# Turning exponentials by a product with diag(1/sum), and the norms' factors moved from x into the weights, in a ten-stage fp32 transformer program

## The chip, the core and the metric

The program runs on one core of one Trainium2 chip. The metric is device time in microseconds of a whole execution. The kernel before takes 2619.73 us, the median of three runs (2615.45 to 2620.55 us). The execution that the profiler recorded took 2619.76 us; its span, from the first instruction to the last, is 2617.6 us. The mean granted clock of TensorE over that span is 0.982 of full speed.

## The reference

Two blocks of two transformer layers run one after the other over 256 tokens of 1024 features, all in fp32. In the first block a context of 256 tokens is carried along with the latent ones through the first layer. What matters here are the attentions, since in each of them a matrix of exponentials is normalised by its row sums and multiplied by values. Cut to that:

```python
# first block, layer 0 (mixer_ab): two attentions over 256 tokens and 256 context tokens
y_x = concat([attention(qa, [ka, ka_c], [va, va_c], 64 ** -0.5),      # 8 heads, 2 K/V heads, 64 wide
              attention(qb, [kb, kb_c], [vb, vb_c], 96 ** -0.5)])     # 8 heads, 96 wide, latent K/V
y_c = the same for the context's queries over the context's keys
# layer 1 (mixer_cd): a gated recurrence, and attention over an 8x16 window of the grid plus the context
p   = softmax(concat([q @ k_win * scale + bias, q @ k_ctx * scale]))
# second block, layer 0: three branches of sparse attention, 12 heads in 3 groups, and 4 memory heads
out = g[0] * softmax(q @ k_cmp) @ v_cmp + g[1] * softmax(q @ k_sel) @ v_sel + g[2] * softmax(q @ k_win) @ v_win
mem = softmax(q_mem @ k_mem * scale) @ v_mem                          # 256 memory tokens
# layer 1: K and V from one norm of x, the queries from another
k_s, v_s = split(rmsnorm(x, kv_norm) @ w_kv_shared)
q, q_mem = split(rmsnorm(x, attn_norm[1]) @ b_w_in)                   # three dilation patterns, 8 heads
out = sum over the patterns of (softmax(q_i @ k_i) @ v_i) weighted by softmax(logsumexp_i)
mem = as above
```

Here `rmsnorm(x, g) = x * rsqrt(mean(x^2) + eps) * g`. Between the mixers stand feed-forward blocks (SwiGLU 2816 wide in the first block, squared ReLU 4096 wide in the second).

## The kernel before

**Stages.** The program is ten stages in a row: modulation with the first feed-forward, `mixer_ab`, a feed-forward, another, `mixer_cd`, the opening of the memory, a feed-forward, the sparse mixer with its memory attention, an MLP, the dilated mixer with its memory attention, an MLP. The residual `xr` stays transposed in SBUF, with the features on the partitions, in eight chunks of 128.

**Products.** A large product is done in three products of rounded parts (`mm3`, lines 328 to 330): high by high, high by low, low by high. `split` makes the two halves, a cast on ScalarE (L300) and a subtraction on VectorE (L301). Weights come by DMA into `raw` (three buffers, issued on SP's queue) and are split into tiles `wh` and `wl` of up to 512 columns, nine of each. `proj_steps` (L719) runs a projection: for each tile of 128 tokens it collects eight chunks of 1024 features in a PSUM bank and then calls `evict`.

**Exponentials.** `softmax` (L836) takes scores of 128 queries from a PSUM bank `at`: the row maxima on VectorE (L841), the exponentials with their row sums on ScalarE (L848), the reciprocal of the sums and then the scaling of each row block by it on VectorE (L859). The scaled block `P` lies with queries on the partitions. `attend_steps` turns it by TensorE transposes of 128x128 against the identity `ident` (L888) into the bank where the scores stood; the result is copied to `PT` by ScalarE or VectorE in turn (L896, L898) and multiplied by the values (`po`, L904). The score product of a head pair is L880, and L810 is the helper `transposes` (its transpose is L814), which turns any list of blocks. The window attention does the same with four blocks of 128 per head (L934, values at L945). In the sparse mixer two maps per head are scaled, `np` (the window's branch on the earlier keys) on POOL and `P` on VectorE (L2030), by gate over sum, and are then turned (L2040 to L2044). In the dilated mixer POOL adds the three patterns' exponentials (L2251, L2252), VectorE scales the sum (L2255), and `transposes` turns it.

**The dilated mixer's input.** Before its projections `gain_split` (L1605) runs 16 times, one ScalarE copy with a factor (L1608) and one VectorE operation (L1609) of 256 columns each: eight chunks times two norms' gains. The tokens multiplied by the gain of the keys' norm lie in columns 256 to 511 of `xh` and `xl`, those of the queries' norm in columns 0 to 255. The root-mean-square factor is applied when a projection is evicted. The projections come in the order `d_k`, `d_q0`, `d_q1`, `d_q2`, `d_qm` (memory queries, 256 columns), `d_v`.

**Order.** The mixers' code is written as generators; a main stream of projections or output products calls `step`, which runs the other stream (a pair of heads, say) up to its next `yield`. This sets the order in which instructions are recorded. The framework then places them on the engines' queues, in which each engine runs in order. Tiles come from pools of rings: a tile name with n buffers makes the instruction that fills buffer n+1 wait for the last reader of buffer 1.

## Time and profile before

| | us |
|---|---|
| median of three runs | 2619.73 (2615.45 to 2620.55) |
| the profiled execution, whole | 2619.76 |
| its span, first to last instruction | 2617.6 |
| TensorE busy in it | 2504.4 (96%) |
| VectorE busy | 1794.8 (69%) |
| ScalarE busy | 1255.3 (48%) |
| POOL busy | 408.5 (16%) |

The engines run beside one another, so these do not add up to the span. A busy engine is not one that sets the end: that is read from the chain of waits, which goes back from the last instruction to what released it, and so on. Both are averages over ten stages with different limits, so the views used below are cut to stretches: the first mixer's pairs run at 450 to 650 us, the window attention at 1550 to 1690, the memory attention of the sparse mixer within 1900 to 1950, the sparse attention at 1980 to 2110, the dilated mixer's projections at 2320 to 2360 and its pairs with the second memory attention at 2360 to 2430. An F32 product of two plain tiles can leave more records in the trace than instructions in the code, so both are counted below.

### The profile page before, as it was taken

The numbers are of one execution on the slowest core, as the hardware profiler recorded it, in microseconds if no ns is written. First come the engines' busy times: TensorE is split into PE (matmuls) and PEld (weight loads), VectorE is DVE, ScalarE is ACT, GpSimd is POOL, SyncE is SP. The second block draws the span as 40 slices with busy tenths as digits, with TensorE's granted clock in tenths as the row PEclk, the third lists the DMA queues.
The fourth block names the chain that finished last, engine by engine and source line by source line (L and its number), as shares of the span: only waits on it lengthen the run. The fifth ranks groups of instructions, "written<-read, shape, count | busy, mean of one in ns | idle before, by whom it ended". The sixth has DMA issues, their size and how long they took to land.

```text
span 2617.6 us, 40598 instructions
## 1 busy us (share of the span) xinstructions
PE 2504.4 (96%) x14835; PEld 2158.1 (82%) x14835; DVE 1794.8 (69%) x3656; ACT 1255.3 (48%) x2641; POOL 408.5 (16%) x457
## 2 busy tenths in 40 slices
PE   6999999999999999999999999889998899988999
PEld 3888888877888888788888887789986789977999
DVE  4999536786998335843336578866677776788764
ACT  3332235665423234233235668555555655665653
POOL 3000004201200003000003234220022211232111
PEclk8999999999999999999999999989998999999999
DMA  7777332110675333843333221346662255542554
GB/s 268 232 234 234 122 96 67 55 60 30 210 237 180 97 97 125 290 131 97 97 97 105 89 81 45 98 136 197 185 189 74 85 181 182 185 142 69 182 184 143
DMA packets 114472, 367.21 MB, mean 140 GB/s; under 512 B 13600, under 2 KB 23776, under 8 KB 112864
## 3 DMA queue, kind: packets, MB, share of 16 engines
q1 hardware_dynamic: 114272, 364.61, 43.4%
q8 instruction: 117, 1.92, 0.3%
q14 instruction: 83, 0.68, 0.1%
HBM read 363.51 MB, written 1.05 MB: 139 GB/s over the span
## 4 chain that ended last, share of the span: by engine, by line
PE 72%; DVE 12%; issue 5%; ACT 5%; DMA 4%; POOL 3%; SPq 0%; POOLq 0%; DVEq 0%; ACTq 0%
PE ps L329 21%; PE ps L330 21%; PE ps L328 21%; DVE wl L301 2%; DVE prod L446 2%; DMA raw<-w 1%; PE po L904 1%; PE at L880 1%; POOL acc L520 1%; PE at L888 1%; ACT wh L300 1%; PE at L814 1%; DMA ident<-c_ident 1%; DVE xl L569 1%; DVE nu L562 1%
## 5 line engine op out<-in xcount | busy, mean ns | idle before, releaser
L300 ACT CAST wh<-raw 128x512 fp32r<-128x512 f32 (+3 forms) x1064 | 637.3, 608 | 914.8 <-PE ps L329 750.6
L301 DVE TENSOR_TENSOR wl<-raw,wh 128x512 fp32r<-128x512 f32 (+3 forms) x1064 | 740.4, 704 | 426.8 <-ACT wh L300 411.7
L328 PE MATMUL ps<-xh,wh 128*128 128x256 f32 (+1 forms) x2384 | 793.8, 336 | 16.9 <-ACT xh L300 5.0
L329 PE MATMUL ps<-xl,wh 128*128 128x256 f32 (+1 forms) x2384 | 796.5, 335 | 10.4 <-POOL xl L573 3.8
L330 PE MATMUL ps<-xh,wl 128*128 128x256 f32 (+1 forms) x2384 | 792.6, 333 | 0.9 <-DVE wl L301 0.9
L328 PEld LDWEIGHTS ps<-xh,wh 128*128 128x128 f32 x2384 | 456.2, 193 | 64.0 <-ACT xh L300 7.1
L329 PEld LDWEIGHTS ps<-xl,wh 128*128 128x128 f32 x2384 | 458.4, 192 | 59.1 <-DVE xl L569 7.2
L330 PEld LDWEIGHTS ps<-xh,wl 128*128 128x128 f32 x2384 | 458.3, 192 | 44.1 <-DVE wl L301 2.1
L328 PE MATMUL ps<-hh,wh 128*128 128x256 f32 (+1 forms) x1312 | 416.5, 318 | 3.7 <-ACT hh L300 3.7
L329 PE MATMUL ps<-hl,wh 128*128 128x256 f32 (+1 forms) x1312 | 416.6, 318 | 0.7 <-DVE hl L301 0.6
L330 PE MATMUL ps<-hh,wl 128*128 128x256 f32 (+1 forms) x1312 | 416.0, 317 | 0.0
L520 POOL TENSOR_TENSOR acc<-acc,sq 128x256 f32<-128x256 f32 x119 | 100.4, 846 | 1375.7 <-ACT sq L519 1371.2
L446 DVE CUSTOM_DVE_ANT_0 prod<-aw,crow,adab 128x1024 f32<-128x1024 f32 x224 | 286.8, 1280 | 7.8 <-DMA aw<-ada_t 5.6
L328 PEld LDWEIGHTS ps<-hh,wh 128*128 128x128 f32 x1312 | 248.0, 189 | 21.7 <-ACT hh L300 4.6
L329 PEld LDWEIGHTS ps<-hl,wh 128*128 128x128 f32 x1312 | 247.9, 189 | 18.7 <-DVE hl L301 1.7
L330 PEld LDWEIGHTS ps<-hh,wl 128*128 128x128 f32 x1312 | 247.9, 189 | 16.8
L328 PE MATMUL ps<-wh,xh 128*128 128x512 f32 (+4 forms) x464 | 180.4, 389 | 1.5 <-ACT xh L1608 1.5
L329 PE MATMUL ps<-wl,xh 128*128 128x512 f32 (+4 forms) x464 | 177.9, 384 | 3.5 <-DVE wl L301 3.5
L330 PE MATMUL ps<-wh,xl 128*128 128x512 f32 (+4 forms) x464 | 176.9, 382 | 0.3 <-DVE xl L1609 0.3
L592 DVE SCALAR_TENSOR_TENSOR xr<-ps,hgate,xr 128x256 f32<-128x256 f32 x168 | 75.5, 479 | 74.4 <-PE ps L330 73.8
L329 PEld LDWEIGHTS ps<-wl,xh 128*128 128x128 f32 x464 | 88.7, 191 | 20.2 <-DVE wl L301 6.5
L300 ACT CAST hh<-s 128x256 fp32r<-128x256 f32 (+1 forms) x158 | 76.9, 487 | 57.5 <-DVE s L642 49.0
(496 smaller groups left out, 2702.8 us busy)
## 6 DMA issues: line engine op xcount, KB each, us to landing
raw<-w SPq DMA_DIRECT2D x240, 512.0 KB, 3.7
aw<-ada_t SPq DMA_DIRECT2D x128, 512.0 KB, 4.1
raw<-m_up SPq DMA_DIRECT2D x64, 512.0 KB, 3.6
raw<-m_down SPq DMA_DIRECT2D x64, 512.0 KB, 3.5
raw<-w SPq DMA_DIRECT2D x32, 384.0 KB, 4.0
row<-ada_w SPq DMA_DIRECT2D x8, 1024.0 KB, 12.9
raw<-d_q SPq DMA_DIRECT2D x12, 512.0 KB, 4.0
raw<-ab_g SPq DMA_DIRECT2D x8, 512.0 KB, 3.6
```

The lines of the kernel that those rows point to most:

```text
L300: self.nc.scalar.copy(h, src)
L301: self.nc.vector.tensor_tensor(l, src, h.bitcast(F32), op=ALU.subtract)
L328: mm(out, lh, rh, start=start, stop=False)
L329: mm(out, lh, rl, start=False, stop=False)
L330: mm(out, ll, rh, start=False, stop=stop)
L446: v.tensor_tensor_reduce(prod, w, self.crow[:, s], 1.0, self.adab[:, l, j : j + 1], op0=ALU.mult, op1=ALU.add, accum_out=self.mods[l][:, m ...
L520: self.nc.gpsimd.tensor_tensor(acc, acc, t, op=ALU.add)
L562: nc.vector.scalar_tensor_tensor(u, self.xr[half][:, k], a[:, k : k + 1], rb, op0=ALU.mult, op1=ALU.mult)
L569: nc.vector.scalar_tensor_tensor(l, u, b[:, k : k + 1], h.bitcast(F32), op0=ALU.add, op1=ALU.subtract)
L592: self.nc.vector.scalar_tensor_tensor(x, pt, gate[:, d : d + 1], x, op0=ALU.mult, op1=ALU.add)
L814: self.nc.tensor.transpose(pt[:rows, n * P : (n + 1) * P], x, self.ident)
L880: nc.tensor.matmul(o, s, kp, start=n == 0, stop=n == len(passes) - 1)
```

## The change

`softmax` no longer scales the exponentials. It calls `diagonals`, which makes for each row block a 128x128 tile `dg`, the identity with 1/sum in its diagonal, as a copy on ScalarE with a scale per partition. `turn` is a plain F32 product of the block (stationary) with that diagonal (moving); the result is the block turned and scaled at once. All transposes of exponentials in the four mixers and both memory attentions become such products, and the scalings on VectorE, and POOL's in the sparse mixer, go. In the sparse mixer a diagonal holds gate over sum. There are 160 diagonals and 384 turns: 192 turns in the first mixer, 64 in the window attention, 16 in each memory attention, 72 in the sparse and 24 in the dilated one.

The `dg` tiles are a new ring: 5 buffers of 128 columns in the first mixer, 3 of 128 in the second, 4 of 256 in the sparse and in the dilated one. Tables of the rotary embedding (`tq`, `tk`), and in the sparse mixer four small tiles of the compression, now lie in that ring too.

In the dilated mixer x is split once, without a gain, into columns 0 to 255: eight casts and eight subtractions in place of 16 and 16. The two norms' gains go into the weights: `weight(gain=...)` makes the high part as a ScalarE copy with the gain as factor and the low part by one VectorE operation, weight times gain minus high part. The features of a weight chunk lie on the partitions, so the factor is one number per partition. That holds for all the mixer's projections, 40 splits of 512 columns and 8 of 256. The weights of `d_qm` are now cut in tiles of 256 columns and not of 512, so that each tile has one gain.

```diff
+    def weight(self, ap, cut=512, gain=None):
...
-            self.split(h, l, r[:, c0 : c0 + m])
+            if gain is None:
+                self.split(h, l, r[:, c0 : c0 + m])
+            else:
+                g = gain[:, c0 // cut : c0 // cut + 1]
+                self.nc.scalar.activation(h, r[:, c0 : c0 + m], AF.Copy, scale=g)
+                self.nc.vector.scalar_tensor_tensor(
+                    l, r[:, c0 : c0 + m], g, h.bitcast(F32), op0=ALU.mult, op1=ALU.subtract
+                )
...
-        ws = [self.weight(u, 512 // ncols * ncols) for u in units]
         kp = kc // len(units)
+        if gain is None:
+            ws = [self.weight(u, 512 // ncols * ncols) for u in units]
+        else:
+            ws = [self.weight(u, ncols, gain[:, kp * n : kp * n + kp]) for n, u in enumerate(units)]
...
         nc.vector.reciprocal(z[:, 2 : 2 + nq], z[:, :nq])
-        for j in range(nq):
-            c = slice(j * nk, (j + 1) * nk)
-            nc.vector.tensor_scalar(pt[:, c], pt[:, c], z[:, 2 + j : 3 + j], None, op0=ALU.mult)
+        return self.diagonals(z[:, 2 : 2 + nq])
+
+    def diagonals(self, z):
+        n, per = z.shape[-1], self.DG_COLS // P
+        ds = []
+        for j in range(n):
+            if j % per == 0:
+                t = self.mw.tile([P, self.DG_COLS], F32, name="dg", tag="dg", bufs=self.DG_BUFS)
+            ds.append(t[:, j % per * P : (j % per + 1) * P])
+            self.nc.scalar.activation(ds[-1], self.ident, AF.Copy, scale=z[:, j : j + 1])
+        return ds
+
+    def turn(self, out, x, d):
+        self.nc.tensor.matmul(out, x, d, start=True, stop=True)
...
-                            nc.tensor.transpose(
-                                tp[:, c : c + P], p[:, j * nk + kk * P : j * nk + (kk + 1) * P], self.ident
-                            )
+                            self.turn(tp[:, c : c + P], p[:, j * nk + kk * P : j * nk + (kk + 1) * P], ds[j])
...
-                        self.bmul(p0, p0, z[:, 8:10])
-                        for b in range(2):
-                            nc.vector.tensor_scalar(p1[:, b], p1[:, b], z[:, 10 + b : 11 + b], None, op0=ALU.mult)
+                        ps.append((p0, p1, self.diagonals(z[:, 8:12])))
...
         for k in range(KC):
-            for g, c0 in ((12, 256), (7, 0)):
-                self.gain_split(self.xr[0][:, k], k, self.gv[:, g], c0)
+            self.split(self.xh[:, k, :256], self.xl[:, k, :256], self.xr[0][:, k])
+        gkv, gq = self.gv[:, 12], self.gv[:, 7]
...
                     nc.vector.reciprocal(z[:, 2:4], z[:, 0:2])
-                    for t, x in enumerate(pp):
-                        nc.vector.tensor_scalar(x[:, 0], x[:, 0], z[:, 2 + t : 3 + t], None, op0=ALU.mult)
+                    ds.append(self.diagonals(z[:, 2:4]))
...
-                    ta = self.transposes([pp[0][:, 0], pp[1][:, 0, :P], pp[1][:, 0, P:]])
+                    ta = self.psum(tag="at")[:, : 3 * P]
+                    for n, (x, d) in enumerate(((pp[0][:, 0], d0), (pp[1][:, 0, :P], d1), (pp[1][:, 0, P:], d1))):
+                        self.turn(ta[:, n * P : (n + 1) * P], x, d)
...
-            self.proj(self.units("d_k"), 512, (2, 3), heads(kx, "k", tk, kd))
+            self.proj(self.units("d_k"), 512, T2, heads(kx, "k", tk, kd), gain=gkv)
...
-                self.proj_steps(self.units("d_qm"), 256, T2, ev_m),
-                self.proj_steps(self.units("d_v"), 512, (2, 3), ev_v),
+                self.proj_steps(self.units("d_qm"), 256, T2, ev_m, gain=gq),
+                self.proj_steps(self.units("d_v"), 512, T2, ev_v, gain=gkv),
```

How instructions stand on the engines is shown at three places. First TensorE in the first mixer, where a projection (`ps`, from split weights `wh`, `wl` and tokens `xh`, `xl`) runs between the steps of the first head pair; `at` is the bank of scores and turned blocks. Before:

```order
L328 MATMUL ps<-wh,xh 128x416
L329 MATMUL ps<-wl,xh 128x416
L330 MATMUL ps<-wh,xl 128x416
L888 MATMUL at<-ident,P 128x128 x4
L880 MATMUL at<-q_3903,q_4029 128x512 x2
L328 MATMUL ps<-wh,xh 128x416
L888 MATMUL at<-ident,P 128x128 x4
L329 MATMUL ps<-wl,xh 128x416
```

And of the change:

```order
L336 MATMUL ps<-wh,xh 128x416
L337 MATMUL ps<-wl,xh 128x416
L338 MATMUL ps<-wh,xl 128x416
L888 MATMUL at<-dg,P 128x128 x4
L909 MATMUL at<-q_3905,q_4031 128x512 x2
L888 MATMUL at<-dg,P 128x128 x4
L336 MATMUL ps<-wh,xh 128x416
```

The turned blocks stand where the transposes stood; the second group of four moved one projection product ahead, and nothing else did. One row is one instruction of the code.

Second ScalarE in the sparse mixer, at the first pair of heads of a group. `np` and `P` are the exponentials of the two maps, `pcT` and `PT` the copies of turned blocks out of PSUM. Before:

```order
L1977 ACTIVATE pc<-pc 128x8x16
L2021 ACTIVATE np_19209,ssum<-np_19209,smax,rq_18309 128x128
L2021 ACTIVATE P,ssum<-P,smax,rq_18309 128x256
L2021 ACTIVATE np_19209,ssum<-np_19209,smax,rq_18309 128x128
L2021 ACTIVATE P,ssum<-P,smax,rq_18309 128x256
L2034 COPY pcT<-at 128x256
L2021 ACTIVATE np_19231,ssum<-np_19231,smax,rq_18309 128x128
L2021 ACTIVATE P,ssum<-P,smax,rq_18309 128x256
L2021 ACTIVATE np_19231,ssum<-np_19231,smax,rq_18309 128x128
L2021 ACTIVATE P,ssum<-P,smax,rq_18309 128x256
L2045 COPY PT<-at 128x512
```

And of the change, the same pair:

```order
L2004 ACTIVATE pc<-pc 128x8x16
L2047 ACTIVATE np_19295,ssum<-np_19295,smax,rq_18391 128x128
L2047 ACTIVATE P,ssum<-P,smax,rq_18391 128x256
L2047 ACTIVATE np_19295,ssum<-np_19295,smax,rq_18391 128x128
L2047 ACTIVATE P,ssum<-P,smax,rq_18391 128x256
L2047 ACTIVATE np_19320,ssum<-np_19320,smax,rq_18391 128x128
L883 ACTIVATE dg<-ident,ssum 128x128 x4
L2047 ACTIVATE P,ssum<-P,smax,rq_18391 128x256
L2047 ACTIVATE np_19320,ssum<-np_19320,smax,rq_18391 128x128
L2047 ACTIVATE P,ssum<-P,smax,rq_18391 128x256
L2058 COPY pcT<-at 128x256
L2067 COPY PT<-at 128x512
```

The four diagonals of the first head now stand behind the first exponential of the second head, so three exponentials and the two copies come after them; four more diagonals, of the second head, follow the last row shown.

Third ScalarE in the dilated mixer, where the memory queries (`qm`) are evicted and the weights of the values (`wh`, the 512-wide casts) are split. Before:

```order
L300 CAST wh<-raw 128x512
L833 CAST qT_22948<-at 64x512
L300 CAST wh<-raw 128x512
L755 ACTIVATE rsy<-ss_23384,cols 128x8
L2170 ACTIVATE qm<-ps,rms 128x256
L756 ACTIVATE rsy<-rsy 128x8
L744 ACTIVATE ps<-ps,rms 128x256
L300 CAST wh<-raw 128x512 x4
L2170 ACTIVATE qm<-ps,rms 128x256
L744 ACTIVATE ps<-ps,rms 128x256
L300 CAST wh<-raw 128x512
```

And of the change:

```order
L848 CAST qT_23053<-at 64x512
L756 ACTIVATE ps<-ps,rms 128x512
L322 ACTIVATE wh<-raw,gv 128x512
L848 CAST qT_23054<-at 64x512
L767 ACTIVATE rsy<-ss_23490,cols 128x8
L768 ACTIVATE rsy<-rsy 128x8
L2192 ACTIVATE qm<-ps,rms 128x256
L756 ACTIVATE ps<-ps,rms 128x256
L322 ACTIVATE wh<-raw,gv 128x512 x4
L2192 ACTIVATE qm<-ps,rms 128x256
L756 ACTIVATE ps<-ps,rms 128x256
L322 ACTIVATE wh<-raw,gv 128x512 x3
```

One more cast of the value weights stands six rows above the first piece, so three of the eight stood ahead of the first eviction of `qm`, four between the two, and one behind. Of the change one stands ahead, four between and three behind. The rows of 512 columns with the factor `gv` are those same splits.

## Rows read from the trace of the kernel before

**Rows 1.** The page: busy time by engine, and the chain that ended last by engine.
```profile
PE 2504.4 (96%) x14835; PEld 2158.1 (82%) x14835; DVE 1794.8 (69%) x3656; ACT 1255.3 (48%) x2641; POOL 408.5 (16%) x457
...
PE 72%; DVE 12%; issue 5%; ACT 5%; DMA 4%; POOL 3%; SPq 0%; POOLq 0%; DVEq 0%; ACTq 0%
```

**Rows 2.** Seven stretches: length, busy us per engine (instructions), TensorE clock, DMA.
```profile
450.00:650.00 200.00, 193.33 (x1135) 152.03 (x1134) 151.07 (x379) 123.73 (x295) 30.61 (x46) 1.00 0.14 45
1550.00:1690.00 140.00, 127.19 (x858) 104.30 (x857) 117.48 (x238) 102.14 (x243) 43.43 (x40) 0.98 0.19 59
1900.00:1950.00 50.00, 49.51 (x308) 42.20 (x306) 36.13 (x100) 25.17 (x53) 13.36 (x18) 1.00 0.59 188
1980.00:2110.00 130.00, 109.20 (x673) 86.33 (x673) 100.60 (x318) 79.76 (x219) 31.23 (x34) 0.89 0.26 82
2260.00:2300.00 40.00, 40.00 (x296) 37.95 (x295) 28.58 (x57) 24.05 (x47) 12.13 (x13) 1.00 0.57 182
2320.00:2360.00 40.00, 36.14 (x192) 29.77 (x191) 38.83 (x76) 27.99 (x61) 13.75 (x10) 1.00 0.40 129
2360.00:2430.00 70.00, 61.69 (x409) 50.29 (x408) 57.47 (x179) 44.48 (x112) 24.98 (x39) 0.99 0.22 69
```

**Rows 3.** Chain of waits by line: 450:650, 1550:1690, 1980:2110, 2320:2360, 2360:2430.
```profile
by line: PE po L904 16.0%; PE ps L328 14.3%; PE ps L329 13.7%; PE ps L330 13.5%; PE at L880 13.0%; PE at L888 10.0%; PE at L814 4.7%; DVE smax L841 2.3%; ACT P L848 1.4%; DVE P L859 1.1%; issue 0.8%; DVE wl L301 0.7%; DVE q L834 0.7%; DVE P
...
by line: issue 5.7%; DVE AT L1472 5.6%; DVE f L1447 4.9%; DVE smax L841 4.4%; PE at L1458 3.9%; PE ps L330 3.8%; PE ps L328 3.7%; PE ps L329 3.5%; PE po L945 3.5%; ACT t L1256 3.1%; ACT t L1258 2.9%; ACT t L1257 2.8%; ACT P L848 2.5%; PE at
...
by line: PE ps L328 6.6%; PE ps L329 6.5%; PE ps L330 5.9%; PE at L1958 5.5%; PE po L2056 5.0%; ACT P L2021 4.3%; issue 4.1%; ACT np L2021 4.0%; PE po L2053 3.9%; PE at L1999 3.9%; ACT xh L1608 3.1%; ACT wh L300 3.0%; DVE wl L301 3.0%; PE a
...
by line: DVE wl L301 34.0%; DVE qT L834 15.6%; issue 10.8%; DVE ss L745 8.4%; DVE x L778 5.2%; DVE P L797 5.0%; DVE x L773 4.8%; DVE kT L301 4.7%; DVE x L805 4.3%; DVE ss L757 3.0%; DVE rsy L345 1.8%; DVE rsa L344 1.4%; DVE rsa L343 1.3%; A
...
by line: issue 13.7%; POOL acc L520 7.9%; DMA raw<-m_up 7.7%; POOL dp L2252 7.4%; PE at L2233 7.2%; POOL dp L2251 6.8%; DVE dp L2239 6.2%; DVE wl L301 5.7%; DMA raw<-d_wout 3.7%; ACT wh L300 3.4%; PE po L904 3.2%; ACT xh L1608 2.9%; PE po L
```

**Rows 4.** TensorE by form: shapes, xcount | busy us, mean ns | idle before.
```profile
L888 PE MATMUL at<-ident,P 128*128 128x128 f32 x224 | 35.0, 277 | 4.4 <-DVE P L859 3.6 <-ACT P L848 0.2
...
L1458 PE MATMUL at<-f,kk 128*128 128x128 f32 x256 | 34.4, 277 | 0.8 <-DVE AT L1472 0.8
```

**Rows 5.** Timeline of TensorE: start us, us from first start to last end, xcount.
```profile
1477.66 0.61 PE L1458 MATMUL at<-f,kk 128*128 128x128 f32 x4
...
1568.14 0.60 PE L934 MATMUL at<-ident,P 128*128 128x128 f32 x4
```

**Rows 6.** Waits of TensorE, 450:650: us in total, times, longest.
```profile
PE at L888 <- DVE P L859: 2.1, 3, 1.2
```

**Rows 7.** VectorE by form, the scalings by 1/sum.
```profile
L859 DVE TENSOR_SCALAR P<-P,ssum 128x512 f32<-128x512 f32 x48 | 24.9, 518 | 1.0
...
L859 DVE TENSOR_SCALAR P<-P,ssum 128x256 f32<-128x256 f32 x48 | 16.0, 376 | 0.4
...
L2030 DVE TENSOR_SCALAR P<-P,ssum 128x256 f32<-128x256 f32 x24 | 11.6, 526 | 0.3
...
L2255 DVE TENSOR_SCALAR dp<-dp,ssum 128x128 f32<-128x128 f32 x8 | 4.0, 498 | 0.5 <-POOL dp L2252 0.3
...
L2255 DVE TENSOR_SCALAR dp<-dp,ssum 128x256 f32<-128x256 f32 x8 | 3.5, 432 | 2.3 <-POOL dp L2252 2.3
```

**Rows 8.** ScalarE by form, the nearest to a diagonal.
```profile
L2021 ACT ACTIVATE np<-np,smax,rq 128x128 f32<-128x128 f32 x24 | 11.7, 486 | 6.4 <-DVE smax L2015 5.0 <-DVE ssum L2025 1.4
...
L1448 ACT ACTIVATE kk<-f,sides 128x256 f32<-128x256 f32 x32 | 16.2, 513 | 2.8 <-PE at L1458 1.3 <-DVE f L1447 1.2
...
L519 ACT ACTIVATE sq<-xr 128x256 f32<-128x256 f32 x105 | 42.8, 413 | 55.5 <-DVE xr L592 40.6 <-POOL acc L520 7.9 <-DVE ssv L531 2.3
...
L1423 ACT COPY state<-at 128x64 f32<-128x64 f32 x8 | 1.7, 213 | 4.0 <-PE at L1416 4.0
```

**Rows 9.** VectorE by form: a weight's low part, and a low part with a factor.
```profile
L301 DVE TENSOR_TENSOR wl<-raw,wh 128x512 fp32r<-128x512 f32 x984 | 701.0, 719 | 418.9 <-ACT wh L300 404.1 <-PE ps L330 7.2
...
L1552 DVE SCALAR_TENSOR_TENSOR q<-at,gqk,q 128x512 fp32r<-128x512 f32 x4 | 3.0, 746 | 0.4 <-ACT q L1551 0.4
```

More of the change, by code (lines that the diff above doesn't have):

```diff
@@ L758, in rstd_heads, with rope_tabs @@
         return self.newton(y, a, ss)
-    def rope_tabs(self, pool, name, tab, g, gs, scale):
+    def rope_tabs(self, pool, name, tab, g, gs, scale, bufs=None, whole=False):
         hd = tab.shape[-1]
-        o = pool.tile([P, 2, 2, hd], F32, name=name)
+        if whole or bufs is None:
+            o = pool.tile([P, 2, 2, hd], F32, name=name, tag=name, bufs=bufs or 1)
+        else:
+            o = [pool.tile([P, 2, hd], F32, name=name, tag=name, bufs=bufs) for _ in range(2)]
         for j, gg in enumerate((g, gs)):
             self.nc.vector.scalar_tensor_tensor(
-                o[:, j], tab[:, j], scale, gg.unsqueeze(1).to_broadcast([P, 2, hd]), op0=ALU.mult, op1=ALU.mult
+                o[:, j] if whole or bufs is None else o[j], tab[:, j], scale, gg.unsqueeze(1).to_broadcast([P, 2, hd]), op0=ALU.mult, op1=ALU.mult
             )
@@ L1914, in compress @@
                 nc.vector.tensor_tensor(kc, kc, tcmp[:, 0], op=ALU.mult)
-                kc2 = mw.tile([64, 2, 64], F32, name="kc2")
+                kc2 = tile("dg", [256], 4)[:64, :P].rearrange("p (b c) -> p b c", b=2)
                 for b in range(2):
```

58 lines of the change are left out of this document (27 added, 31 removed).

## The prediction

> **What bounds the kernel now.** I read the page first: TensorE is busy 96% of the span and makes up 72% of the chain that ended last, VectorE 12% of it [rows 1]. That is an average over stages, so the next view was busy time by stretch [rows 2], for the places where exponentials are turned: the first mixer's pairs (450 to 650 us), the window attention (1550 to 1690), the two memory attentions (in 1900 to 1950, and in 2360 to 2430), the sparse attention (1980 to 2110) and the dilated one (2360 to 2430). Last I read the chain of waits of those stretches alone [rows 3]. The reader is to see that they have different limits:
>
> - First mixer: seven TensorE rows hold 16.0 + 14.3 + 13.7 + 13.5 + 13.0 + 10.0 + 4.7 = 85.2% of the chain. The turning itself (L888) is 10.0% of 200 us. TensorE idles 6.7 us of 200. Paced by TensorE.
> - Window attention: VectorE and ScalarE rows of the recurrence stand between TensorE rows of under 4% each. Paced by hops between engines.
> - Sparse attention: the listed TensorE rows make up 37% of the chain, the exponentials on ScalarE 8.3%, and the rest is spread. The granted clock is 0.89 [rows 2].
> - Projections of the dilated mixer (2320 to 2360): VectorE is busy 38.83 of 40 and holds nearly the whole chain, 34.0% of it in splitting weights.
> - Dilated pairs: POOL's sums of exponentials (L2251, L2252) are 14.2%, and the scaling waits for them [rows 3, 7].
>
> **What an edit costs.** *A turn.* The transposes of lines 888, 934 and 2040 to 2044, and those of the dilated pairs (by the helper of line 814), become 384 products of F32 with a diagonal: 192 in the first mixer, 64 in the window attention, 32 in the memory attentions (16 and 16), 72 in the sparse and 24 in the dilated one. A transpose leaves one record: L888 stands 224 times in the trace, as often as the code issues it. A product of two F32 tiles leaves two: L1458 issues 4 pairs x 8 levels x 4 = 128 products of this form, and the trace has 256 records of the same shape and the same 277 ns [rows 4]. Four records in a row take 0.60 us as transposes and 0.61 us as product halves, so each further one costs (0.61 - 0.28) / 3 = 0.11 us either way [rows 5]. A turn as a product is thus one record longer, and all of them together are 384 x 0.11 = 42 us of TensorE work, an upper end if nothing hides it. The chain gives the same price from the other side: 20.0 us for 192 transposes is 0.104 us each [rows 3].
>
> The Trainium skill, page "TensorE: Matmul & The Clock Gate", section Terms, says that the transpose mode is 4 times as fast for FP32. By that a turn would gain three records and not one. The two records of L1458 say two times; the rule has its own rival below.
>
> *A scaling that goes.* VectorE loses 48 x 518 + 48 x 376 + 24 x 526 + 8 x 498 + 8 x 432 ns = 63 us as means, of which the rows count 24.9 + 16.0 + 11.6 + 4.0 + 3.5 = 60 us as busy [rows 7]; by stage 28.6 us in the first mixer, 8.3 in the window attention, 12.6 in the sparse one, 7.4 in the dilated one, 6.0 in the memory attentions. But TensorE waited for it little: 2.1 us in the whole first mixer [rows 6].
>
> *A diagonal that comes.* The trace has none. ScalarE's nearest rows are a 128x64 copy without a scale pointer at 213 ns (below) and a 128x128 exponential with its sum at 486 ns (above). A scale pointer costs 513 - 413 = 100 ns at 256 columns [rows 8]; the copy plus 64 columns at (413 - 213) / 192 ns plus the pointer gives 0.38. I take 0.4 us, 160 times: 64 us of ScalarE, 26 of them in the first mixer, 19 in the sparse attention, 6.4 each in the window attention, the dilated pairs and the memory attentions. It starts after the same reciprocal that the scaling followed. For a 512-wide row 0.4 takes the place of 0.518. For a sparse head four diagonals (1.6 us, one after the other) take the place of two VectorE scalings (1.05 us) beside POOL's. What is queued behind a waiting diagonal is the next exponential and the PSUM copies that turned tiles wait for.
>
> **The sum, stage by stage.**
>
> - First mixer: 20.0 us of transposes double, and 85.2% of the chain is TensorE, so 0.852 x 20.0 = 17.0; the rest fits into waits that exist. The scaling's 1.1% of the chain goes: -2.2. Place by place the turns stand in the queue where the transposes stood, so nothing moves to a better place. **+15** (between -2 and +21).
> - Window attention: 64 x 0.11 = 7.0 on TensorE, 6.4 on ScalarE, which is already busy 102 of 140, and 8.3 off VectorE, busy 117 of 140. Each is on the chain part of the time. **+2** (-8 to +13).
> - Memory attention before the sparse one: 16 turns in a stretch where TensorE is busy 49.51 of 50: **+1.8**; the second one goes with the dilated pairs.
> - Sparse attention: 72 x 0.11 = 7.9 at 37% of the chain is +2.9; 19 us of ScalarE at 14% (L2021, L1608, L300) is +2.7; 12.6 us of VectorE at about a quarter is -3.1. **+2.5** (-13 to +27).
> - The eight saved splits of x: 8 of the 16 pairs of one ScalarE and one VectorE operation. They fall in 2260 to 2300, where TensorE is busy 40.00 of 40 [rows 2]. **0**; the cover is the tail of the MLP and the products of the first key columns. Without it they would be worth one 256-wide operation each, 8 x 0.5 = -4.
> - The weights' factors: 40 splits 512 wide and 8 of 256 in place of 4 of 512. A low part with a factor takes 746 ns against 719 [rows 9], though the first reads PSUM; I take +50 ns, 40 x 0.05 = 2 us on the engine that paces 2320 to 2360, and 1 us for four operations more. Then there is a wait: the memory queries now fill 8 of the 9 weight buffers and not 4, so the value columns' splits move back. ScalarE's order shows one of eight ahead of the first query eviction where three stood, and three behind the second where one stood. Two splits of 0.72 us late is about 1. **+4** (0 to +8).
> - Dilated pairs with the second memory attention: the scaling no longer stands between POOL's sum and the turn, 0.43 to 0.5 us for each of 16 tiles in four overlapping pairs, against 40 x 0.11 = 4.4 of TensorE. **-2** (-10 to +5).
>
> That is 15 + 2 + 1.8 + 2.5 + 0 + 4 - 2 = +23.3. The profiled execution took 2619.76 us around a span of 2617.6, and the median of the runs is 2619.73, so the sum needs no correction: **2643 us**.
>
> **The rivals.**
>
> - *VectorE is the bound of the attentions (faster).* For it: 117 of 140 and 100.6 of 130 us busy in the window and the sparse attention [rows 2]. If the 8.3, 12.6 and 7.4 us all come off the path, the time is 2620 - 28.3 + 15 + 1.8 + 4 = 2612. It decides from the point where the freed time of VectorE on the chain exceeds TensorE's 17 us in the first mixer. Against it: TensorE's waits name the scaling for 2.1 us there [rows 6]. 0.14.
> - *TensorE's extra records fit into its waits (no change).* The first mixer has 14.8% of 200 = 29.6 us of chain off TensorE, more than 20. For that the waits would have to come when turns are ready; they come in front of them. Then +0 to +4: 2620 to 2624. 0.13.
> - *ScalarE's queue ends last (slower still).* Its diagonals wait in order for VectorE's reciprocal and hold back exponentials. All 42 us of TensorE show and 6 to 7 more from the sparse and window attentions: 2619.8 + 42 + 7 = 2669. 0.17.
> - *A transpose is four times as fast as a product:* 384 x 3 x 0.11 = 127 us more TensorE, 85% of it seen: about 2728. The 256 records of L1458 speak against it. 0.01. The page named above has the rule.
> - *The change does not do what it says:* products with a diagonal run as one record. Then only the VectorE savings and ScalarE's load are left, 2612 to 2618. L1458 speaks against it. 0.03.
>
> **How the numbers follow.** The forecast, 2630 to 2658 by the bounds of the stages that carry it, has 0.52; the rivals have the chances written with them. A measurement of this kernel can tell about 0.2% (5 us) from no change. Slower by more than that: 0.52 + 0.17 + 0.01 = 0.70; within: 0.13; faster: 0.14 + 0.03 = 0.17. The range must leave out no more than 0.2, so it takes in the ScalarE case above and reaches down to the VectorE case: 2611 to 2668.
>
> **What would show it.** In the changed kernel the turns must leave 768 records at about 277 ns, and TensorE's busy time must rise. The stretch of the first mixer must be some 15 us longer, with the turns near 20% of its chain, and the scalings must be gone. The diagonals should read 0.3 to 0.45 us, 160 times. The eight x splits must show no shorter stretch around 2260 to 2300. In the dilated projections a low part of a weight must read about 0.77 us and the wait in front of the value columns must be longer. The prediction is wrong if the first mixer is not longer (the turns were hidden), if a turn leaves one record, or if the sparse stage changes by more than 10 us in either direction.

## Result and the profile after

The changed kernel takes 2652.65 us (median of four runs, 2650.36 to 2656.54) against 2620.14 us of the kernel before in the same runs: a ratio of 1.0128, interval 1.0112 to 1.0144, so 32.5 us slower. The profiled execution has a span of 2648.6 us, 31.0 more than before's 2617.6.

The page of the changed kernel, busy time and chain, answers to [rows 1]:

```profile
PE 2541.4 (96%) x15219; PEld 2200.8 (83%) x15219; DVE 1748.1 (66%) x3516; ACT 1304.6 (49%) x2797; POOL 392.5 (15%) x445
...
PE 74%; DVE 9%; ACT 5%; DMA 5%; issue 4%; POOL 2%; SPq 0%; POOLq 0%; DVEq 0%; ACTq 0%
```

TensorE has 15,219 - 14,835 = 384 records more, exactly one for each turn, and 37.0 us more busy time. VectorE is 46.7 us less busy, ScalarE 49.3 more, and on the chain TensorE has gone from 72% to 74% and VectorE from 12% to 9%.

**Where the time went.** The three-pass products are the same in every kernel here: 4,176 first products each. So the k-th of them is a milestone, and the delay of a stage is how much later its last milestone starts, less how much later its first one does. In each kernel one milestone before the first mixer's pairs and one behind them, from TensorE's timelines (before, then the changed kernel; start, duration):

```profile
450.84 0.48 PE L328 MATMUL ps<-wh,xh 128*128 128x512 f32 x1
...
647.52 0.28 PE L328 MATMUL ps<-xh,wh 128*128 128x256 f32 x1
```

```profile
450.00 0.48 PE L336 MATMUL ps<-wh,xh 128*128 128x512 f32 x1
...
664.77 0.28 PE L336 MATMUL ps<-xh,wh 128*128 128x256 f32 x1
```

Delay at the first pair is 450.00 - 450.84 = -0.84, at the second 664.77 - 647.52 = +17.25, so the first mixer's pairs cost +18.1. By before's time the milestones stand at 450.8 and 647.5 us (first mixer), 1554.0 and 1752.4 (window attention), 1935.2 and 1976.6 (memory attention), 1976.6 and 2129.0 (sparse attention), 2288.1, 2353.0 and 2448.6 (dilated mixer: projections, then pairs; the products of the value columns start at 2353.0 and so count with the pairs). The same at all of these, in us, with the twelve kernels described below, each against the kernel before:

| kernel | first mixer | window | memory | sparse | dilated, projections | dilated, pairs | elsewhere | span |
|---|---|---|---|---|---|---|---|---|
| the change | +18.1 | +4.4 | +1.2 | +8.1 | +1.9 | +0.2 | -3.0 | +31.0 |
| e1_records | +20.5 | +7.8 | +1.6 | +7.4 | -0.1 | -0.2 | -1.2 | +35.7 |
| e2_diag_transpose | -0.8 | -4.8 | -0.2 | +14.8 | +0.2 | -0.6 | -1.1 | +7.5 |
| e3_turns_only | +17.9 | +4.4 | +0.8 | +8.3 | +0.4 | +0.9 | -3.4 | +29.1 |
| e4_dil_only | +0.2 | -0.1 | +0.2 | +0.1 | +2.5 | -1.4 | -1.8 | -0.4 |
| e5_diag_vector | +19.6 | +5.2 | +1.8 | +14.6 | +1.5 | +0.2 | -1.7 | +41.2 |
| e6_diag_pool | +33.2 | +14.2 | +6.2 | +21.8 | +1.8 | +2.8 | -9.3 | +70.7 |
| e7_turn_twice | +60.2 | +20.5 | +7.4 | +20.6 | +1.6 | +9.0 | -1.2 | +118.2 |
| e8_qm_plain | +18.0 | +5.1 | +4.1 | +8.1 | +0.6 | +1.7 | +1.5 | +39.0 |
| e9_sparse_product | -0.8 | -3.4 | -0.6 | +8.2 | -0.4 | 0.0 | -2.0 | +0.9 |
| e10_window_scale | +0.2 | -2.7 | +0.3 | -0.2 | -0.4 | -1.4 | +0.8 | -3.4 |
| e11_idle_records | +0.1 | -0.7 | -0.3 | +3.3 | +0.2 | -2.0 | -2.2 | -1.5 |
| e12_transpose_twice | -0.9 | -3.0 | -0.1 | +12.1 | +0.2 | -1.9 | +3.4 | +9.8 |

"Elsewhere" is what none of these edits touches. It moves by a few microseconds from one execution to the next (by -9.3 in e6), so a total from one profile says less than the stages. In stages that an edit leaves alone the values mostly stay within 1.5 us (the memory attention of e8, +4.1 with the same code as the change's +1.2, and the dilated pairs of e11, -2.0, do not). The pairs of e10 and e11, whose code is before's, stand at -1.4 and -2.0, so before's own profiled execution was probably long there by 1 to 2 us.

Stretches of the changed kernel that answer to [rows 2] (same columns), with their starts and ends moved along:

```profile
450.00:667.00 217.00, 213.94 (x1318) 176.00 (x1317) 132.88 (x315) 143.67 (x358) 28.73 (x45) 1.00 0.13 42
1564.00:1710.00 146.00, 134.69 (x926) 112.58 (x925) 109.06 (x222) 106.69 (x260) 43.83 (x40) 0.98 0.18 59
2000.00:2140.00 140.00, 117.98 (x762) 96.22 (x762) 92.45 (x298) 94.64 (x268) 23.38 (x24) 0.91 0.24 78
2289.00:2329.00 40.00, 40.00 (x295) 37.95 (x295) 26.59 (x49) 21.85 (x39) 10.09 (x13) 1.00 0.53 173
2349.00:2390.00 41.00, 37.58 (x195) 29.66 (x194) 39.10 (x74) 30.51 (x63) 15.07 (x12) 1.00 0.38 125
```

By the milestones the first mixer is 18.1 us longer; TensorE is busy 213.94 of the 217 us shown. In the sparse attention VectorE has fallen from 100.60 of 130 to 92.45 of 140 and the stage is longer all the same. Around the x splits (fourth row) TensorE still never pauses.

The chain of waits by line, first mixer and sparse attention, answers to the first and third of [rows 3]:

```profile
by line: PE at L888 19.7%; PE po L931 14.0%; PE at L909 13.2%; PE ps L336 11.5%; PE ps L337 11.3%; PE ps L338 11.2%; PE at L829 3.7%; DMA raw<-ab_ukv 2.2%; DMA raw<-ab_wout 1.6%; DVE wl L301 1.6%; ACT wh L300 1.1%; ACT P L864 1.0%; DVE ss L
...
by line: PE at L888 8.1%; ACT dg L883 7.2%; ACT P L2047 5.8%; PE ps L336 5.4%; ACT np L2047 5.3%; DMA mc<-memT 5.2%; PE ps L338 4.9%; PE at L1985 4.8%; PE ps L337 4.5%; PE at L2026 4.1%; issue 4.1%; PE po L2078 3.0%; DVE xl L1636 2.8%; PE p
```

The turn has gone from 10.0% of 200 us to 19.7% of 217, that is from 20.0 to 42.7 us. In the sparse attention the diagonals are now on the chain, 7.2% of 140 = 10 us, in the scalings' place.

New and changed instructions by form (shapes, count | busy us, mean ns | idle before), to be read beside [rows 4, 7 to 9]:

```profile
L888 PE MATMUL at<-dg,P 128*128 128x128 f32 x672 | 95.5, 284 | 7.1 <-ACT dg L883 6.8
...
L883 ACT ACTIVATE dg<-ident,ssum 128x128 f32<-128x128 f32 x160 | 56.3, 396 | 7.8 <-DVE ssum L872 5.4 <-DVE ssum L2053 1.4 <-DVE ssum L2275 0.8
L323 DVE SCALAR_TENSOR_TENSOR wl<-raw,gv,wh 128x512 fp32r<-128x512 f32 x40 | 33.1, 839 | 3.1 <-ACT wh L322 3.0
L322 ACT ACTIVATE wh<-raw,gv 128x512 fp32r<-128x512 f32 x40 | 27.6, 721 | 9.2 <-PE ps L338 3.9 <-PE ps L337 3.5 <-DMA raw<-d_v 1.3
...
L888 PE MATMUL at<-dg,np 128*128 128x128 f32 x48 | 9.8, 287 | 0.0
...
L888 PE MATMUL at<-dg,dp 128*128 128x128 f32 x48 | 6.8, 274 | 0.0
```

672 + 48 + 48 = 768 records for 384 turns, of the length of a transpose's. A diagonal takes 0.396 us. The low part of a weight with its factor takes 839 ns against 719, more than the 0.77 us that the prediction named.

### The profile page after: what moved, and what is told of

It reads as the page before. It is cut to its first block, busy times and chain, and to the rows that moved or that the text cites. A ratio compares the mean times of both kernels' runs of the same rounds, so it can differ in the third digit from the quotient of the medians.

```text
span 2648.6 us, 41320 instructions
## 1 busy us (share of the span) xinstructions
PE 2541.4 (96%) x15219; PEld 2200.8 (83%) x15219; DVE 1748.1 (66%) x3516; ACT 1304.6 (49%) x2797; POOL 392.5 (15%) x445
## 4 chain that ended last, share of the span: by engine, by line
PE 74%; DVE 9%; ACT 5%; DMA 5%; issue 4%; POOL 2%; SPq 0%; POOLq 0%; DVEq 0%; ACTq 0%
PE ps L337 22%; PE ps L336 21%; PE ps L338 21%; PE at L888 3%; DVE wl L301 1%; PE po L931 1%; PE at L909 1%; DMA raw<-w 1%; POOL acc L528 1%; ACT wh L300 1%; DMA aw<-ada_t 1%; DMA ident<-c_ident 1%; DVE wl L323 1%; PE at L829 1%; DVE prod L454 1%
## 5 line engine op out<-in xcount | busy, mean ns | idle before, releaser
L300 ACT CAST wh<-raw 128x512 fp32r<-128x512 f32 (+2 forms) x1020 | 611.7, 607 | 909.9 <-PE ps L337 753.3
L301 DVE TENSOR_TENSOR wl<-raw,wh 128x512 fp32r<-128x512 f32 (+2 forms) x1020 | 705.1, 699 | 430.8 <-ACT wh L300 416.8
L337 PEld LDWEIGHTS ps<-hl,wh 128*128 128x128 f32 x1312 | 248.1, 189 | 18.1 <-DVE hl L301 1.2
```

What stands on the lines that cost most here:

```text
L300: self.nc.scalar.copy(h, src)
L301: self.nc.vector.tensor_tensor(l, src, h.bitcast(F32), op=ALU.subtract)
L337: mm(out, lh, rl, start=False, stop=False)
```

## Experiments

The theory (R): what the change costs is TensorE's second record of each turn. The first rival (S): ScalarE's diagonals, and what waits behind them, cost it. The first four kernels take the change apart: the second record alone, the diagonals alone, both together, and the dilated mixer's input alone.

**e1_records.** The kernel before, with products against the identity in place of transposes:

```diff
-                nc.tensor.transpose(tp[:, kk * P : (kk + 1) * P], p[:, kk * P : (kk + 1) * P], self.ident)
+                self.turn(tp[:, kk * P : (kk + 1) * P], p[:, kk * P : (kk + 1) * P])
...
+    def turn(self, out, x):
+        self.nc.tensor.matmul(out, x, self.ident, start=True, stop=True)
```

> The kernel before with one edit: every turn of exponentials is a plain F32 product with the identity in place of a transpose. The scalings on VectorE and POOL stay, no diagonal is made. Theory R (the added time is TensorE's second record of each turn): 2643 to 2652 us; by stage against before about +16 in the first mixer, +4 in the window attention, +1 in the sparse mixer's memory attention, +8 in the sparse attention, 0 to +3 in the dilated mixer. Rival S (the added time is ScalarE's diagonals and what waits behind them): the records fit into waits, under 2630, with at most +5 in the first mixer and +2 in the sparse attention.

Measured: 2656.28 us, ratio 1.0144 (1.0127 to 1.0161); by stage as in the table. More than the forecast range of R by 4 us in all, and R by stage: +20.5 of 192 x 0.11 = 21.1 us of new records in the first mixer, +7.8 of 7.0 in the window, +1.6 of 1.8 in the memory attention, +7.4 of 7.9 in the sparse one, and none that shows of the 4.4 in the dilated pairs and their memory attention. The first mixer and the window lie above R's +16 and +4. S falls as the account of the whole: without one diagonal the kernel is as slow as the change.

**e2_diag_transpose.** The change's attentions with the diagonals, turned by one-record transposes:

```diff
-        nc.vector.reciprocal(z[:, 2 : 2 + nq], z[:, :nq])
+        nc.vector.tensor_tensor(z[:, 2 : 2 + nq], z[:, :nq], z[:, :nq], op=ALU.is_equal)
...
-        self.nc.tensor.matmul(out, x, d, start=True, stop=True)
+        self.nc.tensor.transpose(out, x, d)
```

> The changed kernel with transposes of one record against the diagonals, and with the dilated mixer's input as before. So that a transpose can take them, the diagonals hold 1 and not 1/sum: the reciprocal is a comparison of the sum with itself, of the same size on the same engine. It leaves out the division by the sums and two of the sparse mixer's gates; the diagonals are made and waited for as in the change. Theory R: 2615 to 2624 us, no stage further than 3 us from before. Rival S: 2635 or more, with the sparse attention 6 or more longer than before. If VectorE's scalings had been on the path, 2600 to 2612.

Measured: 2627.23 us, ratio 1.0036 (1.0022 to 1.0050). This fits neither. In the first mixer and the window attention the exchange of scalings for diagonals is worth -0.8 and -4.8 us (-3.4 and -3.0 in the window attention of e9 and e12, which have the same code there). In the sparse attention it costs 14.8, more than the change with its second records does. Of the six executions of e2 the shortest, 2621.21 us, has the highest mean granted clock, 0.982, and the longest, 2631.99, the lowest, 0.976; the profiled one took 2626.88 at 0.977. e9 and e12 follow that up.

**e3_turns_only.** The change without its edit of the dilated mixer's input:

```diff
-            self.split(self.xh[:, k, :256], self.xl[:, k, :256], self.xr[0][:, k])
+            for g, c0 in ((12, 256), (7, 0)):
+                self.gain_split(self.xr[0][:, k], k, self.gv[:, g], c0)
...
-            self.proj(self.units("d_k"), 512, T2, heads(kx, "k", tk, kd), gain=gkv)
+            self.proj(self.units("d_k"), 512, (2, 3), heads(kx, "k", tk, kd))
```

> The changed kernel with the dilated mixer's input as before: x is split twice with the two gains, the weights without a factor. Diagonals and products as in the change. Theory R with the forecast's term for the weights: 2648 to 2651, so 2 to 4 us under the change, all of it gained before the dilated pairs. Rival (the saved splits of x are worth their time): 2653 to 2657.

Measured: 2649.58 us, ratio 1.0124 (1.0109 to 1.0139) beside the change's 1.0128: the two can't be told apart by their times. By stage its projections cost +0.4 and the change's +1.9, so 1.5 us went where the forecast put them; e3's pairs were 0.7 longer.

**e4_dil_only.** The counterpart: the kernel before with the change's `weight(gain=...)` and one split of x.

```diff
-            for g, c0 in ((12, 256), (7, 0)):
-                self.gain_split(self.xr[0][:, k], k, self.gv[:, g], c0)
+            self.split(self.xh[:, k, :256], self.xl[:, k, :256], self.xr[0][:, k])
...
-            self.proj(self.units("d_k"), 512, (2, 3), heads(kx, "k", tk, kd))
+            self.proj(self.units("d_k"), 512, T2, heads(kx, "k", tk, kd), gain=gkv)
```

> The kernel before with the dilated mixer's input of the change alone: x split once, the gains as factors of the weights' splits, memory query weights in tiles of 256. Transposes and scalings as before. Forecast's term: 2622 to 2625 (+2 to +4), all of it between the last MLP product before the dilated mixer and the dilated pairs; a low part of a weight 0.1 us longer than before. Rival (the saved splits are worth their time): 2612 to 2618. Rival (the wait of the value weights for buffers is the price): +5 or more, with TensorE waiting in front of the value columns.

Measured: 2620.79 us, ratio 1.0017 (1.0008 to 1.0026); +2.5 in the projections, -1.4 in the pairs. That is just under the 2622 to 2625 named, and 3.6 over the kernel before in the same runs (2617.15). The forecast's term holds in size. The saved splits gain nothing: in e4 every milestone from 2231 to 2299 us, where the splits run, stands at the same -0.6 against before, and in the change at the same +28.9.

**e5_diag_vector and e6_diag_pool.** Who should make the diagonals?

```diff
-            self.nc.scalar.activation(ds[-1], self.ident, AF.Copy, scale=z[:, j : j + 1])
+            self.nc.vector.tensor_scalar(ds[-1], self.ident, z[:, j : j + 1], None, op0=ALU.mult)
```

(`gpsimd` in place of `vector` in e6.)

> The changed kernel with the 160 diagonals made on VectorE, a scaling of the identity by 1/sum, 128 columns each, in place of ScalarE copies. Turns as in the change. Theory R (TensorE's records are the price, ScalarE's diagonals are beside them): within 3 us of the change, 2649 to 2656, the sparse attention no more than 2 us from its +8. Rival S (ScalarE's queue of diagonals, exponentials and PSUM copies sets the sparse attention): the sparse attention 4 to 8 us shorter than in the change, 2642 to 2647 in all.

> The changed kernel with the 160 diagonals made on POOL, which is idle in most of these stretches. A diagonal should read 0.4 to 0.9 us there. Theory R: the first mixer, paced by TensorE, moves by less than 3 us whoever makes the diagonals; where engines wait for one another (window and sparse attention) a later diagonal may cost 0 to +8, 2650 to 2663. Rival S: the sparse attention 4 us or more shorter than in the change, as in the run with VectorE. If the latency of a diagonal sets the first mixer, +8 or more there.

Measured: 2660.52 us, ratio 1.0167 (1.0147 to 1.0187), with VectorE, and 2699.19 us, ratio 1.0310 (1.0283 to 1.0337), with POOL. VectorE makes a diagonal faster than ScalarE and yet lengthens the sparse attention by 6.5 us; S forecast the opposite, and R, which allowed 2 us there and 2656 in all, missed too. With POOL every attention gets longer, the first mixer too, by 15.1 us where R allowed 3: what held is the last condition of the forecast, that the latency of a diagonal can set the first mixer. TensorE's waits for diagonals over the whole span (us, times, longest), in the change, in e5 and in e6:

```profile
PE at L888 <- ACT dg L883: 6.8, 9, 1.9
```

```profile
PE at L888 <- DVE dg L883: 9.8, 8, 2.2
```

```profile
PE at L888 <- POOL dg L883: 40.2, 37, 4.2
```

So TensorE can be held up by a diagonal that comes late, which 0.4 us on ScalarE rarely does. The diagonals by form, in e5 and in e6:

```profile
L883 DVE TENSOR_SCALAR dg<-ident,ssum 128x128 f32<-128x128 f32 x160 | 45.2, 318 | 1.9
```

```profile
L883 POOL TENSOR_SCALAR dg<-ident,ssum 128x128 f32<-128x128 f32 x160 | 100.2, 636 | 246.2 <-DVE ssum L872 125.8 <-DVE ssum L2053 43.0 <-DVE smax L861 36.5
```

Of the three engines ScalarE makes the diagonals at the least cost to the whole.

**e7_turn_twice.** The dose doubled, 768 records more than the change:

```diff
         self.nc.tensor.matmul(out, x, d, start=True, stop=True)
+        self.nc.tensor.matmul(out, x, d, start=True, stop=True)
```

> The changed kernel with every turn issued twice, the second product over the first: 768 records more, 84 us of TensorE at 0.11 us each. Theory R: nearly all of it shows where TensorE sets the pace, +38 to +43 in the first mixer, +3 to +4 in the memory attention before the sparse one; +9 to +14 in the window attention, +10 to +16 in the sparse attention, 0 to +5 in the dilated mixer: 2713 to 2735. Rival (the records fit into waits and the change's price has another source): under 2690.

Measured: 2732.66 us, ratio 1.0448 (1.0426 to 1.0471). The span grew by 118.2 - 31.0 = 87.2 us over the change for 84 us of records: +42.1 in the first mixer for 42.2 of records, +16.1 in the window for 14.1, +12.5 in the sparse attention for 15.8, +8.8 in the dilated pairs for 8.8, and +6.2 in the memory attention for 3.5, where e8 shows how far single executions scatter. The window and the memory attention and the dilated pairs lie above what was expected. Taken together, a record costs its full 0.11 us.

**e8_qm_plain.** The memory queries' weights in four tiles again:

```diff
-                self.proj_steps(self.units("d_qm"), 256, T2, ev_m, gain=gq),
+                self.proj_steps(self.units("d_qm"), 256, T2, ev_m),
```

> The changed kernel with the memory queries' weights split as before, in four tiles of 512 without a factor; it leaves the norm's gain out of the memory queries. The value columns' splits then find buffers earlier. Forecast's term (two splits late is about 1 us): 2650 to 2653, with 1 us less between the dilated mixer's first projection and its pairs. Rival (the wait for buffers is most of the dilated mixer's price): 3 us less there.

Measured: 2653.57 us, ratio 1.0135 (1.0106 to 1.0163), the same as the change. Its projections cost +0.6 against +1.9, so the wait for buffers is about 1.3 us. That agrees with the forecast's 1, though it is no larger than the scatter of stages; and what was won is lost in the pairs behind. The starts of the projections' products say where it lies: from first to last those of the memory queries take 6.0 us before and in e3, 7.2 in the change and in e4 and 6.5 here, while those of the value columns take 13.0 before, 13.1 in the change and 15.0 here. So about 1 us comes in the memory queries' own columns, and the value columns, where the prediction put the wait, are not longer.

**e11_idle_records.** The forecast had weighed TensorE's work by its share of the chain. Here are as many records as the change adds to the sparse attention, where nobody waits for them:

```diff
                         for n in range(2):
                             nc.tensor.matmul(s1[e], q[:, P:], k[:, n], start=n == 0, stop=n == 1)
+                        if e:
+                            po = self.psum(tag="po")[:, :256]
+                            for n in range(6):
+                                nc.tensor.matmul(po[:, :P], q[:, :P].bitcast(F32), self.ident, start=True, stop=True)
...
-                    po = self.psum(tag="po")[:, :256]
```

> The kernel before with 36 F32 products of 128x128 more in the sparse attention, 72 records of 0.11 us: as many as the change adds there, but put beside the scores, into a bank that nothing reads until the value products overwrite it, so that no engine waits for them. Theory C (a record is paid in full because the turn lies between exponential and values, where all wait): these are hidden in part, +1 to +4 in the sparse attention. Rival T (TensorE's queue is full there): +7 to +8, as with the second record of the turns.

Measured: 2620.47 us, ratio 1.0010 (1.0000 to 1.0019); +3.3 us in the sparse attention. The records, by form:

```profile
L2003 PE MATMUL po<-ident,nq 128*128 128x128 f32 x72 | 10.9, 302 | 0.0
```

72 records beside the scores cost 3.3 us, 72 records between exponentials and values 7.4 (e1). The clock does not make the difference: between the milestones of that stage it is 0.91 before and in e11, and 0.93 in e1. Theory C holds, on one profiled execution of each kernel.

**e9_sparse_product and e12_transpose_twice.** Both are e2 with one edit in the sparse attention: products (e9, shown), or in `turn2` two transposes in a row (e12).

```diff
-                            self.turn(s0[:, 256 * e + b * P : 256 * e + (b + 1) * P], p1[:, b, 1], ds[2 + b])
+                            self.turn2(s0[:, 256 * e + b * P : 256 * e + (b + 1) * P], p1[:, b, 1], ds[2 + b])
...
+    def turn2(self, out, x, d):
+        self.nc.tensor.matmul(out, x, d, start=True, stop=True)
```

> The run with one-record transposes against diagonals of 1 (division and gates left out as there), with one edit: in the sparse attention alone the turns are F32 products, two records each. There the transposes had cost 14.8 us over before with TensorE at half clock for 47.8 us of the two longest stretches. Theory (the clock falls where TensorE does less): the sparse attention gets shorter with more records, +8 to +10 over before, half clock for 20 to 30 us, 2617 to 2623 in all. Rival (diagonals cost 15 us there by themselves and records come on top): +18 to +23, 2628 to 2636.

> As the run with F32 products in the sparse attention alone (division and gates left out as there), but each turn of the sparse attention is issued as two transposes in a row, one record each. So TensorE has as many records there as with the products, of the same 0.11 us, and only their kind differs. Theory (a transpose does not keep the clock up as a product does): half clock for 40 us or more within the sparse attention, +13 or more over before there. Rival (any TensorE work of that length keeps it up): half clock for 20 to 30 us, +7 to +9, as with the products.

Measured: e9 2620.15 us, ratio 1.0009 (1.0000 to 1.0018), with +8.2 in the sparse attention; e12 2622.75 us, ratio 1.0020 (1.0010 to 1.0030). The profiled execution of e12 was its longest, 2629.27 us, with +12.1 there, so its times count for more than its profile. The same 112 us of the three kernels (e2, e9, e12; columns as in [rows 2], the third figure from the end is the granted clock):

```profile
1975.00:2087.00 112.00, 87.26 (x494) 66.10 (x493) 63.27 (x242) 71.09 (x215) 9.55 (x8) 0.76 0.16 52
```

```profile
1975.00:2087.00 112.00, 93.17 (x621) 75.92 (x619) 70.22 (x255) 76.95 (x230) 14.26 (x13) 0.89 0.18 56
```

```profile
1975.00:2087.00 112.00, 92.63 (x580) 73.27 (x579) 66.05 (x249) 71.66 (x215) 10.86 (x9) 0.85 0.17 54
```

e9's theory holds: with more records the stage is 6.6 us shorter than e2's, at a clock of 0.89 and not 0.76, and the ratios of the whole kernels, 1.0009 and 1.0036, have intervals that do not meet. On e12's question, whether the kind of record matters, the answer is open: the clock with twice the transposes lies at 0.85, nearer to the products, and the time lies between the two.

**e10_window_scale.** e2 had gained 4.8 us in the window attention, so one scaling of two was moved off VectorE there, with the transposes as before:

```diff
+            if act:
+                nc.scalar.activation(pt[:, c], pt[:, c], AF.Copy, scale=z[:, 2 + j : 3 + j])
+            else:
...
-                self.softmax(sc, ps[-1], 1, 512)
+                self.softmax(sc, ps[-1], 1, 512, act=len(ps) == 2)
```

> The kernel before with one edit in the window attention: of its two heads the second one's exponentials are scaled on ScalarE (a copy with the factor, 512 columns) and not on VectorE, eight scalings. Transposes as before. With diagonals in place of scalings the window attention got 5 us shorter where a turn was one record. Theory (VectorE's scaling is on the path there): 1 to 4 us shorter than before, 2612 to 2619. Rival (ScalarE is as full as VectorE): within 1 us or longer.

Measured: 2616.92 us against 2618.55, ratio 0.9993 (0.9985 to 1.0002). The window attention is 2.7 us shorter, as forecast. Its granted clock between the milestones is 0.97 and was 0.95, so a part of the 2.7 may be the clock's (the change and e3, at 0.97 and 0.95, take the same +4.4 there). The whole kernel can't be told from the one before. None of these kernels is clearly faster than it.

## Why the forecast was right, and where it was short

The direction and the mechanism held: 2643 us forecast, 2652.65 measured, inside the range. The range, 2611 to 2668, holds faster kernels too, so lying in it says little; the bounds given for the forecast itself, 2630 to 2658, hold the time as well. Of +31.0 in the span the forecast had +23.3. That it came so near is in part luck: the first mixer, the window, the sparse attention and the dilated pairs were each forecast too cheap, by 13.3 us together, the weights' factors and the memory attention too dear by 2.7, and the parts that no edit touches lay 3.0 lower in the profiled execution.

- *A turn leaves one record more, of 0.11 us.* 384 more records, shown by the page and by e1 and e7.
- *First mixer, +15 forecast, +18.1 measured.* The scaling's part, -2.2, fits: e1 keeps the scaling and costs +20.5, the change +18.1 (with one-record turns, in e2, the exchange is worth -0.8). The part that failed is "0.852 x 20.0 = 17.0; the rest fits into waits that exist". Nearly all 21.1 us show, 20.5.
- *Window, +2 forecast, +4.4 measured.* The records cost +7.8 (e1), the exchange of scalings for diagonals gives back 3.4, as it does by itself in e2, e9 and e12 (3.0 to 4.8).
- *Sparse attention, +2.5 forecast, +8.1 measured.* This is the term that was mis-sized most, and in it "72 x 0.11 = 7.9 at 37% of the chain is +2.9". e1 shows +7.4 for that term alone. The 37% were themselves read too low: they add up the rows that the line of [rows 3] shows before it ends, and over the whole chain of that stretch TensorE holds 54%, which would make +4.3, still short. A share of the chain fits such records where nobody waits for them: e11's 3.3 of 7.9 is 42%. But a turn stands between the exponential and the values: TensorE waits there for the scaled exponentials, and the copies and value products behind the turn wait for it. TensorE's waits for the scalings in e1 in that stage (us, times, longest; 3.2 us in the kernel before):

```profile
PE at L863 <- DVE P L2032: 4.1, 4, 1.5
```

and its chain there (138 us), in which the turns, now all on line L863, hold 15.5%, 21 us (before, on the three lines L2040, L2043 and L2044, 6.6% of 130, 8.6 us):

```profile
by line: PE at L863 15.5%; PE ps L328 5.6%; PE ps L330 5.0%; PE ps L329 5.0%; PE po L2056 5.0%; DVE wl L301 4.7%; issue 3.8%; PE at L1960 3.8%; ACT xh L1610 2.9%; PE po L2053 2.9%; PE at L2001 2.9%; ACT wh L300 2.9%; PE po L2059 2.6%; DVE x
```

- *The exchange of VectorE's and POOL's scalings for ScalarE's diagonals in the sparse attention*, -0.4 in the forecast, is +0.7 by the change against e1. Beside one-record transposes it is far dearer (e2). So the two do not add up in that stage: the records alone cost 7.4, the exchange alone 14.8, both together 8.1.
- *Memory attention, +1.8 forecast, +1.2 measured.* The prediction read the wrong stretch: the 16 transposes run at 1952 to 1971 us and not within 1900 to 1950. The term holds all the same, for TensorE is as full at the right place (the kernel before, columns as in [rows 2]):

```profile
1950.00:1977.00 27.00, 26.21 (x146) 18.56 (x145) 21.61 (x56) 17.11 (x45) 11.45 (x14) 1.00 0.54 175
```

- *x splits, 0 forecast*, and TensorE is busy 40.00 of 40 there after the change too.
- *Weights' factors, +4 forecast, +1.9 measured (+2.5 in e4).* The factor costs 120 ns on a low part and not 50, 40 x 0.12 = 4.8 us on VectorE, of which at most half shows. e8 puts the wait for buffers at about 1, but in the memory queries' columns; how the 1.9 divides between the wait and the factor is within the scatter and not shown.
- *Dilated pairs, -2 forecast, +0.2 measured.* Within its bounds. Of the 4.4 us of records little shows in e1 (-0.2; against e10 and e11, which have before's code there, +1 to +2), and the change costs no less than e1, so the freed scalings gave nothing that shows.

The rival with ScalarE's queue is refuted as the cause of the whole by e1, and its remedy by e5; in the sparse attention the diagonals have a price of their own (e2), and how the +8.1 divides there stays open. That with VectorE as the bound is refuted by the change itself (VectorE lost 46.7 us of busy time and the kernel got longer), and that of hidden records by e1 and e7. That the tables moved into the diagonals' ring are the price is refuted by e1 too, which leaves them where they were. The rivals on the number of records are refuted by the 768 records.

## What to carry to other kernels

In this kernel a share of the chain priced the work that nobody waits for. Work that is added between a producer and the consumer that everybody waits for is better priced in full, even on an engine that is idle a sixth of the time, as TensorE is in the sparse attention. Add such a share up over the whole chain and not over the rows that a line has room for. Moving a scaling from VectorE into a TensorE product did not pay here, since the product leaves one record more than the transpose that it replaces; with one-record turns (e2) it did not pay either, for what the window attention gained was lost in the sparse one. Align two traces by instructions that both contain: stage by stage they show single microseconds where the totals of single executions differ by several.

## What the runs showed of the hardware that was not expected

**Fewer records, a longer stage.** In e2 the sparse attention has one record per turn and is 6.6 us longer than in e9 with two. Three stretches of e2 (columns as in [rows 2]):

```profile
1980.00:2012.00 32.00, 23.62 (x93) 17.22 (x93) 20.22 (x64) 15.18 (x44) 4.98 (x5) 0.52 0.18 58
2012.00:2022.00 10.00, 7.11 (x50) 5.59 (x48) 6.65 (x39) 6.08 (x22) 0.00 (x0) 0.99 0.01 3
2022.00:2040.00 18.00, 13.38 (x52) 8.40 (x53) 4.80 (x23) 11.92 (x38) 0.00 (x0) 0.53 0.00 0
```

and of e9, the second and third of these (in the first its clock is low too, 0.63):

```profile
2012.00:2022.00 10.00, 7.79 (x50) 5.95 (x49) 6.54 (x39) 6.75 (x24) 0.00 (x0) 1.00 0.01 3
2022.00:2040.00 18.00, 16.08 (x125) 12.97 (x124) 10.71 (x35) 13.83 (x42) 0.00 (x0) 1.00 0.07 22
```

A granted clock of 0.52 is the 1.2 GHz level for nearly the whole stretch. In e2 TensorE was busy 7.11 of 10 us ahead of 2022 and its clock fell a second time; in e9 it was busy 7.79 and it stayed at 2.4 GHz. In these 18 us e2 ran 52 records, e9 125. These are one execution each, and what tipped the clock between two so similar stretches is not shown. The change has the clock at 0.91 in that stage, before 0.89: its second records cost time and may give back a little of it.

The Trainium skill, page "TensorE: Matmul & The Clock Gate", section "Part 4: PE-mode transpose", says that a transpose does not count towards TensorE being busy as a product does. By that e12 would have e2's clock. Its 0.85 lies between e2's 0.76 and e9's 0.89, so the runs neither confirm the rule nor refute it.

**POOL's diagonal** took 636 ns, VectorE's 318 ns and ScalarE's 396 ns for the same 128x128 tile.
